# Tap products of the last convolution block in a bank of the common pool, issued in four pieces between the attention heads

## The chip, the cores and the metric

The kernel runs on one NeuronCore of a Trainium2 chip. The metric is device time of one launch, in microseconds (us), lower is better. Five engines work side by side, each through its own queue, strictly in order: PE (TensorE, the matrix unit), DVE (VectorE), ACT (ScalarE), POOL (GpSimd) and SP (SyncE, which here only issues transfers). They wait for one another through semaphores, so an instruction whose operand is late also holds up all that stand behind it in its queue.

## The reference, cut to what matters

A two-layer encoder on 512 tokens of width 1024, all in float32. Each layer is a feed-forward block, a mixer, a second feed-forward block and a norm. The mixer projects the normed stream once and splits the columns between eight attention heads and a convolution module:

```python
def conv_group(u_raw, conv_w, conv_b, ln_g, ln_b):
    a, g = u_raw[..., :CONV_W], u_raw[..., CONV_W:]     # CONV_W = 512
    u = a * jax.nn.sigmoid(g)
    y = lax.conv_general_dilated(u, conv_w[:, None, :], window_strides=(1,),
        padding=[(CONV_K - 1, 0)], feature_group_count=CONV_W, ...)   # causal, depthwise, CONV_K = 31
    y = y + conv_b
    return jax.nn.silu(layer_norm(y, ln_g, ln_b))
...
x = x + jnp.concatenate([attn, conv], axis=-1) @ w_out[l]
```

The LayerNorm runs over all 512 convolution channels, so nothing of it can begin before every channel has its 31 taps summed.

## The kernel before, in words

Activations lie with channels on the 128 partitions and the 512 tokens along the free axis, so one 128x512 float32 tile holds 128 channels and fills one PSUM bank. A large product is made of three matmuls (L144, L145, L146) on a rounded high part and a remainder of each operand. ACT makes the high parts of weights (`wh`, L133) and DVE the remainders (`wl`, L139); both have rings of four tiles, and the raw weights a ring of three (`raw`), filled by SP in program order.

PSUM has eight banks. Seven form the common pool `ps`, from which `bank()` takes; a taken bank returns when its last reader is done. The eighth is a pool of its own with one tile, tag `cv`.

The convolution's 512 channels are four blocks, and the string `CONV = "DAAP"` says how each gets its 31 taps:

- Block 0, kind D: an accumulator `cv` in the eighth bank. ACT writes the first tap and the bias (L813), DVE adds the other 30 in a chain, each `scalar_tensor_tensor` reading what the one before wrote (L817), and ACT copies the result out (L827).
- Blocks 1 and 2, kind A: for each tap ACT multiplies (`pr`, L821, three buffers) and POOL adds (`y`, L825), 30 each.
- Block 3, kind P: `packed`. Sixteen small transfers make four tiles (`zs`), each with 32 channels in four copies shifted by 0 to 3 tokens (L783, after a four-column memset, L781). PE then multiplies by 128x32 tap matrices `wtap`: eight steps of four matmuls, one for each group of 32 channels, which write 32 partitions each (L787). The four of a step use separate column strips of the array. The profile counts every such float32 matmul twice. ACT adds the bias (L790). The accumulator is the same `cv` bank that block 0 uses, and `packed` comes first in the program.

The mixer goes through these stages: projections (first two weight tiles of block 0, then q latents, blocks 1 and 2, k latents, queries, keys), the eight heads, the convolution's sum and LayerNorm, the output projection. The heads are software-pipelined in steps: in each step one head is turned (q and k transposed, L695 and L700, copied by ACT L697 and DVE L702), another has its scores made (L718, mask L719, maximum on DVE L720, exponential on ACT L724), another its probabilities transposed (L739, copied out at L742), another its values (L752), and each second head its output transposed (L770). After the turn of step 1 the projection of block 3 is issued, and at the end of step 2 `packed(3)`.

POOL then sums the four blocks (L839, L840, L841; the first adds block 0 to block 1, the last adds block 3), one matmul forms the mean (L843), DVE subtracts it (L849), and the rest of the LayerNorm alternates with the first half of the output projection (L144 to L146, on attention's output).

The order of each engine's queue is not the program's. The tile framework simulates the program with its own costs and writes out a static order per engine, in which an instruction stands as early as its operands and buffers let it be in that simulation. The order thus follows from the buffers, and a change of a buffer moves instructions far away from it.

Of the kernel before, what the change touches and what calls it, by code (L numbers as in the profile page):

```python
# [7 lines left out]
FP = mybir.dt.float32  # L8
# [3 lines left out]
AF = mybir.ActivationFunctionType  # L12
# [3 lines left out]
P = 128  # L16
D = 1024
S = 512
# [52 lines left out]
def encoder_kernel(ctx: ExitStack, tc: tile.TileContext, xT, consts, vecs, rgain, wgu1, wd1,  # L71
# [9 lines left out]
    psum = ctx.enter_context(tc.tile_pool(name="psum", bufs=7, space=PSUM))  # L81
    uid = [0]

    def nm(s):
        uid[0] += 1
        return f"{s}{uid[0]}"

    def slot(dt=FP, w=S):
        return ring.tile([P, w], dt, tag="r", name=nm("r"))
# [4 lines left out]
    def bank():  # L94
        return psum.tile([P, S], FP, tag="ps", name=nm("ps"))
# [4 lines left out]
    V, A, G, T = nc.vector, nc.scalar, nc.gpsimd, nc.tensor  # L100
# [23 lines left out]
    def vv(l, name):  # L124
        o, w = VOFF[name]
        return vec[:, l, o:o + w]
# [373 lines left out]
    def mix(l, gx, norm, done):  # L500
        with tc.tile_pool(name="k", bufs=4) as kpool:
            mix_body(kpool, l, gx, norm, done)

    def mix_body(kpool, l, gx, norm, done):
        u, order = [], {}
        ys = [None if kind in "DP" else kpool.tile([P, S], FP, tag="y", name=nm("y"), bufs=2) for kind in CONV]
# [12 lines left out]
        def conv_in(c):  # L519
            pp = []  # L520
            for j in range(2):
                ps = bank()
                group(ps, load_w(wcv[l, 2 * c + j], WC, f"c{c}"), gx, range(KD), KD)
                pp.append(ps)
            glu(*pp)
# [244 lines left out]
                T.transpose(ps[:, t * P:(t + 1) * P], o[:, t * P:(t + 1) * P], ident)  # L770
            at.append(split(ps))

        def packed(c):

            w = wpool.tile([P, WC], FP, tag="raw", name=nm("raw"), bufs=3)
            nc.sync.dma_start(out=w, in_=wtap[l])
            acc = psum.tile([P, S], FP, tag="cv", name=nm("cv"), bufs=1)
            zs = []
            for g in range(4):
                t = slot()  # L780
                V.memset(t[:, 0:4], 0.0)  # L781
                for j in range(4):
                    nc.sync.dma_start(out=t[32 * j:32 * j + 32, j:S], in_=u[c][32 * g:32 * g + 32, 0:S - j])  # L783
                zs.append(t)
            for i in range(8):
                for g in range(4):
                    T.matmul(acc[32 * g:32 * g + 32, 4 * i:S], w[:, (g * 8 + i) * 32:(g * 8 + i + 1) * 32],  # L787
                             zs[g][:, 0:S - 4 * i], start=i == 0, stop=i == 7, skip_group_check=True)
            y = slot()
            A.activation(y, acc, AF.Identity, bias=cb[:, c:c + 1])  # L790
            ys[c] = y

        cw, cb = vv(l, "cw"), vv(l, "cb")
        STAGES = [({"t": turn, "s": scores, "p": turn_p, "v": values, "o": turn_out}[c], int(d)) for c, d in zip(ORDER[::2], ORDER[1::2])]
        for step in range(H + 6):
            for stage, lag in STAGES:
                if 0 <= step - lag < H:
                    stage(step - lag)
                if stage is turn and step == 1:
                    conv_in(3)  # L800
            if step == 2:
                packed(3)


        with tc.issue_after(order["keys"]):
# [1 line left out]
        for c in range(4):  # L807
# [3 lines left out]
            acc = psum.tile([P, S], FP, tag="cv", name=nm("cv"), bufs=1) if kind == "D" else ys[c]  # L811
# [44 lines left out]
        cv = []  # L856
# [224 lines left out]
```

## Time and profile before

| | us |
|---|---|
| median of three runs | 1876.25 (1876.04 to 1877.94) |
| the profiled execution | 1878.56 |
| its span, first to last instruction | 1876.4 |
| PE busy in it | 1822.6 (97%) |
| DVE busy | 1310.0 (70%) |
| ACT busy | 955.2 (51%) |
| POOL busy | 272.9 (15%) |

The mean granted clock of TensorE is 0.988 of full speed. The layers' mixers lie at about 340 to 570 us and 1270 to 1500 us of the span; their heads at about 443 to 534 and 1372 to 1464.

In a timeline row the first number is the start in us, the second the duration; then engine, source line, operation, output and inputs by the program's names, shapes, and how many instructions the row merges. A bracket at the end tells how long the engine sat idle before it and what ended that. In a table of windows each engine has its busy time and count, and PEclk is the granted clock.

### The profile page before, as it was taken

How to read it: one execution, taken by the hardware profiler on the slowest of the kernel's cores; microseconds unless marked ns; L12 is line 12 of the kernel's file. 1: busy time of each engine (PE TensorE's matmuls, PEld its weight loads, DVE VectorE, ACT ScalarE, POOL GpSimd, SP SyncE). 2: the span in 40 equal slices, each digit the busy share in tenths (PEclk: the TensorE clock that was granted, in tenths of full speed). 3: DMA queues.
4: the chain of work that ended last, by engine and by line, in shares of the span. 5: the costliest groups of instructions: out<-in, count | busy, mean ns of one | idle time of the engine just before them, and what ended most of it. 6: DMA issues, size and time to landing. Idle time of an engine off the chain costs nothing.

```text
span 1876.4 us, 22441 instructions
## 1 busy us (share of the span) xinstructions
PE 1822.6 (97%) x8640; PEld 1497.8 (80%) x8640; DVE 1310.0 (70%) x1751; ACT 955.2 (51%) x1469; POOL 272.9 (15%) x216
## 2 busy tenths in 40 slices
PE   8999999999899999999999999999989999999997
PEld 6888888887578888888877888888957788888885
DVE  8957775648658957767778667864567579578754
ACT  6534444468735644445644344443777446344441
POOL 4000000057812000000000000000686210000000
PEclk9999999999999999999999999999999999999998
DMA  8332322325115333332713332222250343423121
GB/s 288 111 124 80 112 68 67 113 84 141 29 61 165 99 104 112 101 101 66 226 65 97 97 114 89 79 81 95 77 146 12 124 107 111 127 87 120 68 68 56
DMA packets 60315, 191.10 MB, mean 102 GB/s; under 512 B 6576, under 2 KB 7728, under 8 KB 60208
## 3 DMA queue, kind: packets, MB, share of 16 engines
q1 hardware_dynamic: 56320, 176.70, 29.0%
q0 software_dynamic: 3456, 12.58, 3.6%
q8 instruction: 68, 1.11, 0.2%
q10 hardware_dynamic: 432, 0.38, 0.1%
q14 instruction: 39, 0.32, 0.1%
HBM read 185.45 MB, written 2.10 MB: 100 GB/s over the span
## 4 chain that ended last, share of the span: by engine, by line
PE 74%; issue 18%; DVE 4%; ACT 2%; POOL 2%; DMA 0%; SPq 0%; POOLq 0%; DVEq 0%; ACTq 0%
PE ps L144 22%; PE ps L146 22%; PE ps L145 22%; PE ps L752 2%; PE ps L718 2%; PE ps L365 1%; DVE wl L229 1%; PE ps L739 1%; POOL y L825 1%; PE cv L787 0%; PE ps L182 0%; DVE fr L325 0%; ACT pr L821 0%; ACT r L724 0%; PE ps L700 0%
## 5 line engine op out<-in xcount | busy, mean ns | idle before, releaser
L144 PE MATMUL ps<-wh,r 128*128 128x512 f32 (+2 forms) x1392 | 524.8, 387 | 12.2 <-ACT wh L227 8.2
L145 PE MATMUL ps<-wl,r 128*128 128x512 f32 (+2 forms) x1392 | 534.3, 386 | 0.0
L146 PE MATMUL ps<-wh,r 128*128 128x512 f32 (+2 forms) x1392 | 532.0, 385 | 0.0
L227 ACT CAST wh<-fr 128x1024 fp32r<-128x1024 f32 x256 | 269.1, 1052 | 271.8 <-PE ps L146 143.1
L144 PE MATMUL ps<-r,wh 128*128 128x512 f32 x1008 | 393.7, 396 | 0.4 <-ACT r L150 0.4
L146 PE MATMUL ps<-r,wl 128*128 128x512 f32 x1008 | 392.8, 391 | 0.5 <-POOL wl L139 0.5
L145 PE MATMUL ps<-r,wh 128*128 128x512 f32 x1008 | 392.7, 390 | 0.0
L229 DVE TENSOR_TENSOR wl<-fr,wh 128x1024 fp32r<-128x1024 f32 x256 | 314.1, 1229 | 106.1 <-ACT wh L227 105.5
L144 PEld LDWEIGHTS ps<-wh,r 128*128 128x128 f32 x1392 | 262.5, 189 | 62.4 <-ACT wh L227 8.2
L145 PEld LDWEIGHTS ps<-wl,r 128*128 128x128 f32 x1392 | 262.5, 189 | 50.6 <-issue 0.5
L146 PEld LDWEIGHTS ps<-wh,r 128*128 128x128 f32 x1392 | 262.2, 188 | 50.3
L133 ACT CAST wh<-raw 128x1024 fp32r<-128x1024 f32 (+2 forms) x150 | 148.3, 992 | 207.0 <-issue 88.9
L139 DVE TENSOR_TENSOR wl<-raw,wh 128x1024 fp32r<-128x1024 f32 (+3 forms) x134 | 160.3, 1199 | 94.8 <-ACT wh L133 93.8
L144 PEld LDWEIGHTS ps<-r,wh 128*128 128x128 f32 x1008 | 189.8, 189 | 41.7 <-issue 1.5
L145 PEld LDWEIGHTS ps<-r,wh 128*128 128x128 f32 x1008 | 190.2, 189 | 41.1 <-issue 2.0
L146 PEld LDWEIGHTS ps<-r,wl 128*128 128x128 f32 x1008 | 189.9, 188 | 41.3 <-POOL wl L139 1.3
L162 POOL TENSOR_TENSOR rtok<-vtok,minus_half 128x4 f32<-128x4 f32 x9 | 11.1, 1229 | 1094.1 <-DVE vtok L188 1094.1
L443 DVE SCALAR_TENSOR_TENSOR x<-ps,x 128x512 f32<-128x512 f32 x128 | 88.2, 689 | 111.8 <-PE ps L146 111.3
L825 POOL TENSOR_TENSOR y<-y,pr 128x509 f32<-128x509 f32 (+15 forms) x120 | 158.0, 1319 | 56.2 <-ACT pr L821 49.4
L325 DVE TENSOR_TENSOR fr<-fr,fr 128x1024 f32<-128x1024 f32 x112 | 135.7, 1224 | 7.7 <-DMA fr<-in_wgu 7.3
L355 ACT ACTIVATE e<-e,rtok 128x256 f32<-128x256 f32 x120 | 61.2, 511 | 102.6 <-DVE e L346 102.4
L341 ACT COPY e<-ps 128x512 f32<-128x512 f32 x120 | 70.4, 588 | 63.3 <-PE ps L146 63.1
(169 smaller groups left out, 1717.0 us busy)
## 6 DMA issues: line engine op xcount, KB each, us to landing
fr<-in_wgu SPq DMA_DIRECT2D x176, 512.0 KB, 3.9
raw<-in_wd SPq DMA_DIRECT2D x64, 512.0 KB, 4.2
raw<-in_wd SPq DMA_DIRECT2D x32, 384.0 KB, 3.2
raw<-in_wcv SPq DMA_DIRECT2D x16, 512.0 KB, 3.4
raw<-in_wout SPq DMA_DIRECT2D x16, 512.0 KB, 4.3
raw<-in_wgu SPq DMA_DIRECT2D x8, 512.0 KB, 4.5
fr<-in_wgu POOLq DMA_DIRECT2D x8, 512.0 KB, 6.9
raw<-in_wgu POOLq DMA_DIRECT2D x8, 512.0 KB, 7.8
```

The lines of the kernel that those rows point to most:

```text
L133: A.copy(hi[:, :w], raw[:, :w])
L139: (G if kind in POOLW.split() else V).tensor_tensor(lo[:, :w], raw[:, :w], hi[:, :w].bitcast(FP), ALU.subtract)
L144: T.matmul(o, lh, rh, start=first, stop=False, skip_group_check=free)
L145: T.matmul(o, lh, rl, start=False, stop=False, skip_group_check=free)
L146: T.matmul(o, ll, rh, start=False, stop=last, skip_group_check=free)
L227: A.copy(hi[:, :w], src[:, :w])
L229: V.tensor_tensor(lo[:, :w], src[:, :w], hi[:, :w].bitcast(FP), ALU.subtract)
L325: V.tensor_tensor(oh, ah, bh, ALU.add)
L341: A.copy(w[:, j, :N], o[j][:, :N])
L355: A.activation(out[j][:, :h], src[j][:, :h], AF.Silu, scale=r)
L443: V.scalar_tensor_tensor(x[:, m, :], pd, 0.5, x[:, m, :], ALU.mult, ALU.add)
L825: order["conv"] = G.tensor_tensor(acc[:, s:], acc[:, s:], pr[:, s:], ALU.add).ins
```

## The change

`packed` is cut in two. `prepare` loads the tap matrices and issues the memsets and the sixteen shifted copies; it is called at step 1, just after the projection of block 3, where before this stood in `packed` at step 2. Its accumulator is now `bank()`, one of the seven of the common pool, held from step 1 until the bias add. The eight tap steps are issued two at a time, at the ends of steps 3, 4, 5 and 6. Nothing else is written differently. The eighth bank, tag `cv`, is left to block 0 alone.

```diff
+        pk = {}
+
+        def packed(c, steps):
+
+            if not pk:
+                prepare(c)
+            acc, w, zs = pk["acc"], pk["w"], pk["zs"]
+            for i in steps:
+                for g in range(4):
+                    T.matmul(acc[32 * g:32 * g + 32, 4 * i:S], w[:, (g * 8 + i) * 32:(g * 8 + i + 1) * 32],
+                             zs[g][:, 0:S - 4 * i], start=i == 0, stop=i == 7, skip_group_check=True)
+            if steps[-1] < 7:
+                return
+            y = slot()
+            A.activation(y, acc, AF.Identity, bias=cb[:, c:c + 1])
+            ys[c] = y
+
-        def packed(c):
+        def prepare(c):
 
             w = wpool.tile([P, WC], FP, tag="raw", name=nm("raw"), bufs=3)
             nc.sync.dma_start(out=w, in_=wtap[l])
-            acc = psum.tile([P, S], FP, tag="cv", name=nm("cv"), bufs=1)
             zs = []
...
                     nc.sync.dma_start(out=t[32 * j:32 * j + 32, j:S], in_=u[c][32 * g:32 * g + 32, 0:S - j])
                 zs.append(t)
-            for i in range(8):
-                for g in range(4):
-                    T.matmul(acc[32 * g:32 * g + 32, 4 * i:S], w[:, (g * 8 + i) * 32:(g * 8 + i + 1) * 32],
-                             zs[g][:, 0:S - 4 * i], start=i == 0, stop=i == 7, skip_group_check=True)
-            y = slot()
-            A.activation(y, acc, AF.Identity, bias=cb[:, c:c + 1])
-            ys[c] = y
+            pk.update(acc=bank(), w=w, zs=zs)
...
-            if step == 2:
-                packed(3)
+            if step == 1:
+                prepare(3)
+            if 3 <= step < 7:
+                packed(3, (2 * step - 6, 2 * step - 5))
```

Line numbers shift: the tap matmuls are L787 before and L782 after, the memsets L781 and L797, the DVE taps L817 and L829, ACT's products L821 and L833, the bias add L790 and L787. SP's queue holds the same transfers in the same order.

The order moves at three places, shown for layer 0; layer 1 moves in the same way. The first is DVE's queue in the projections. L139 makes remainders of weights, L510, L514 and L516 the gated inputs `r` of the blocks (`r_2947` is block 0's), and `cv` is block 0's accumulator. Before:

```order
L516 TENSOR_TENSOR r_2947<-t_2945,t_2943 128x512
L139 TENSOR_TENSOR wl_3086<-raw_3082,wh_3084 128x1024
L510 TENSOR_TENSOR t_3011<-ps_2980,R_2939 128x512
L514 TENSOR_TENSOR t_3015<-ps_2949,R_2939 128x512
L139 TENSOR_TENSOR wl_3117<-raw_3113,wh_3115 128x1024
L516 TENSOR_TENSOR r_3017<-t_3015,t_3013 128x512
```

And now:

```order
L516 TENSOR_TENSOR r_2947<-t_2945,t_2943 128x512
L829 SCALAR_TENSOR_TENSOR cv_4381<-r_2947,vec,cv_4381 128x511
L829 SCALAR_TENSOR_TENSOR cv_4381<-r_2947,vec,cv_4381 128x510
L829 SCALAR_TENSOR_TENSOR cv_4381<-r_2947,vec,cv_4381 128x509
L139 TENSOR_TENSOR wl_3086<-raw_3082,wh_3084 128x1024
L829 SCALAR_TENSOR_TENSOR cv_4381<-r_2947,vec,cv_4381 128x508
L829 SCALAR_TENSOR_TENSOR cv_4381<-r_2947,vec,cv_4381 128x507
L829 SCALAR_TENSOR_TENSOR cv_4381<-r_2947,vec,cv_4381 128x506
L829 SCALAR_TENSOR_TENSOR cv_4381<-r_2947,vec,cv_4381 128x505
L510 TENSOR_TENSOR t_3011<-ps_2980,R_2939 128x512
L829 SCALAR_TENSOR_TENSOR cv_4381<-r_2947,vec,cv_4381 128x504
L139 TENSOR_TENSOR wl_3117<-raw_3113,wh_3115 128x1024
```

All 30 taps of block 0 now stand here, the last (482 columns wide) just ahead of the splits of the q latents (L157) and of the last two query weights; before, they stood between the heads, from the first scores after the tap matmuls to the last transposes.

The second place is PE's queue among the heads. `cst` is the identity of the transposes, `raw` the tap matrices, `r` after the arrow the shifted copies. Before, the 32 matmuls stand in one run, which begins so:

```order
L739 MATMUL ps_3899<-cst,r_3737 128x128
L739 MATMUL ps_3899<-cst,r_3738 128x128
L739 MATMUL ps_3899<-cst,r_3739 128x128 x2
L787 MATMUL cv_3795<-r_3796,raw_3793 32x512
L787 MATMUL cv_3795<-r_3802,raw_3793 32x512
L787 MATMUL cv_3795<-r_3808,raw_3793 32x512
L787 MATMUL cv_3795<-r_3814,raw_3793 32x512
L787 MATMUL cv_3795<-r_3796,raw_3793 32x508
```

Now the first three stand apart from the fourth, with a head's turn and scores between:

```order
L719 MATMUL ps_3834<-mneg,mrow 128x64
L782 MATMUL ps_3782<-r_3758,raw_3756 32x512
L782 MATMUL ps_3782<-r_3764,raw_3756 32x512
L695 MATMUL ps_3885<-cst,q_2814 96x128 x4
L700 MATMUL ps_3892<-cst,kn_2815 96x128 x4
L718 MATMUL ps_3899<-r_3832,r_3825 128x128
L719 LDWEIGHTS mrow
L719 MATMUL ps_3899<-mneg,mrow 128x64
L782 MATMUL ps_3782<-r_3770,raw_3756 32x512
```

In whole, the 32 stand in eight runs of 2, 1, 12, 2, 7, 4, 1 and 3, each between matmuls of the heads.

The third place is ACT's queue. `pr` are products of block 2, L697 copies a head's turned queries, L724 is the exponential. Before, fifteen products follow each other, with no exponential between, up to the bias add L790:

```order
L821 ACTIVATE pr_4536<-r_3149,vec 128x501
L821 ACTIVATE pr_4539<-r_3149,vec 128x500
L790 ACTIVATE r_3852<-cv_3795,vec 128x512
L697 ACTIVATE r_3859<-ps_3854,gqs_3632 96x512
L724 ACTIVATE r_3873,sums_3871<-ps_3868,mx_3872 128x128
L724 ACTIVATE r_3874,sums_3871<-ps_3869,mx_3872 128x384
```

Now the same products stand among the exponentials of the heads:

```order
L833 ACTIVATE pr_4527<-r_3149,vec 128x504
L697 ACTIVATE r_3965<-ps_3960,gqs_3632 96x512
L833 ACTIVATE pr_4530<-r_3149,vec 128x503
L724 ACTIVATE r_3979,sums_3977<-ps_3974,mx_3978 128x128
L724 ACTIVATE r_3980,sums_3977<-ps_3975,mx_3978 128x384
L833 ACTIVATE pr_4533<-r_3149,vec 128x502
L724 ACTIVATE r_3981,sums_3977<-ps_3976,mx_3978 128x512
L833 ACTIVATE pr_4536<-r_3149,vec 128x501
L833 ACTIVATE pr_4539<-r_3149,vec 128x500
```

The bias add now stands eight products later, just ahead of the turn of the last head, and block 0's two ACT instructions (L813, L827) stand in the projections. On PE nothing has moved from the last output transpose (L770) on: the mean's matmul follows it directly in both.

## The prediction

> **What bounds the kernel now.** I read the page first, then PE's timeline through each mixer, then the releasers of its longest waits, then the tables of windows.
>
> ```profile
> span 1876.4 us, 22441 instructions
> ...
> PE 1822.6 (97%) x8640; PEld 1497.8 (80%) x8640; DVE 1310.0 (70%) x1751; ACT 955.2 (51%) x1469; POOL 272.9 (15%) x216
> ```
>
> PE is busy for 97% of the span. A change that adds and removes no arithmetic can gain where PE waits, where its clock is low, or where it runs badly packed. In the two mixers it does all three. First the tap matmuls, PE's timeline in layer 0:
>
> ```profile
> 463.10 0.70 PE L718 MATMUL ps<-r,r 96*128 96x256 f32 x2 [1.46 <-ACT r L724]
> ...
> 470.75 1.05 PE L787 MATMUL cv<-r,raw 128*32 128x512 f32 x2
> 473.00 1.02 PE L787 MATMUL cv<-r,raw 128*32 128x512 f32 x2 [1.20 <-DMA r<-r]
> ...
> 478.06 8.79 PE L787 MATMUL cv<-r,raw 128*32 128x512 f32 x58 [0.75 <-DMA r<-r]
> 486.79 0.44 PE L739 MATMUL ps<-cst,r 128*128 128x128 f32 x2
> 488.21 0.64 PE L695 MATMUL ps<-cst,q 128*96 128x128 f32 x4 [0.98 <-ACT r L697]
> ```
>
> The tap matmuls hold PE's queue from 470.75 to 486.79, 16.04 us: each of the first three waits for its shifted copy, and whatever head could have run stands behind. Then PE waits 0.98 for ACT. Layer 1:
>
> ```profile
> 1398.01 1.04 PE L787 MATMUL cv<-r,raw 128*32 128x512 f32 x2
> ...
> 1405.56 6.84 PE L787 MATMUL cv<-r,raw 128*32 128x512 f32 x58 [1.59 <-DMA r<-r]
> 1412.33 0.44 PE L739 MATMUL ps<-cst,r 128*128 128x128 f32 x2
> 1415.80 0.64 PE L695 MATMUL ps<-cst,q 128*96 128x128 f32 x4 [3.03 <-ACT r L697]
> ```
>
> Here the block takes 1398.01 to 1412.33, 14.32 us, and the wait behind it 3.03. Then the end of the heads in both layers, PE's timeline:
>
> ```profile
> 533.55 0.66 PE L770 MATMUL ps<-cst,t 128*128 128x128 f32 x4 [0.79 <-DVE t L759]
> 537.26 2.07 PE L843 MATMUL ps<-t,onesm 128*128 128x512 f32 x2 [3.05 <-POOL t L841]
> ...
> 1467.06 2.08 PE L843 MATMUL ps<-t,onesm 128*128 128x512 f32 x2 [3.06 <-POOL t L841]
> ```
>
> PE has nothing left but the mean, and that waits for POOL's sum. What the sum waited for stands in the timelines of DVE, ACT and POOL:
>
> ```profile
> 531.85 0.72 DVE L817 SCALAR_TENSOR_TENSOR cv<-r,vec,cv 128x482 f32<-128x482 f32 x1
> ...
> 532.60 0.59 ACT L827 COPY r<-cv 128x512 f32<-128x512 f32 x1 [1.39 <-DVE cv L817]
> ...
> 533.26 1.26 POOL L839 TENSOR_TENSOR t<-r,y 128x512 f32<-128x512 f32 x1 [17.98 <-ACT r L827]
> ...
> 1463.06 1.26 POOL L839 TENSOR_TENSOR t<-r,y 128x512 f32<-128x512 f32 x1 [19.00 <-ACT r L827]
> ```
>
> POOL had blocks 1 and 2 ready 17.98 and 19.00 us earlier; the late one is block 0, whose last tap ends at 532.57. Its accumulator is the bank that the tap matmuls held until 487. Last, a table of windows:
>
> ```profile
> 377.00:412.00 35.00, 35.00 (x176) 30.05 (x175) 13.52 (x13) 19.53 (x28) 21.66 (x15) 1.00 0.22 63
> 443.00:515.00 72.00, 64.59 (x382) 43.36 (x381) 46.45 (x90) 60.35 (x123) 64.47 (x53) 0.93 0.33 81
> 500.00:510.00 10.00, 10.00 (x82) 8.77 (x80) 9.72 (x19) 9.70 (x25) 9.45 (x8) 1.00 0.01 2
> 536.00:544.00 8.00, 6.74 (x15) 4.64 (x16) 4.42 (x7) 2.76 (x6) 1.21 (x1) 0.57 0.00 0
> 1415.00:1425.00 10.00, 9.20 (x43) 6.99 (x43) 5.91 (x11) 10.00 (x26) 7.87 (x8) 0.66 0.02 7
> 1465.00:1475.00 10.00, 7.94 (x23) 5.73 (x24) 4.82 (x8) 3.55 (x6) 1.93 (x2) 0.66 0.00 0
> ```
>
> Columns after the length are PE, its weight loads, DVE, ACT, POOL, then the clock. After three of these waits the clock is 0.57 to 0.66 of full. I price that as PE's busy time times what the clock lacks.
>
> **The change part by part.**
>
> *Tap matmuls.* Price of a pass: 58 counted matmuls in 6.84 us at full clock (layer 1) is 0.118 each, so a step of four channel groups, eight counted matmuls, takes 0.94 us. A single group alone takes 1.04 to 1.05. One pass thus costs about the same whether one or four groups share it. One unbroken run would need 8 passes, 7.5 us. The eight new runs of 2, 1, 12, 2, 7, 4, 1 and 3 need 1+1+3+1+2+1+1+1 = 11 passes, 10.4 us. Against 16.04 and 14.32 that saves 5.65 and 3.9, together 9.5. Bounds: 8 passes, if neighbours overlap the broken ones, save 15.2; if each of the eight runs also pays a lone group of 1.05 more, a layer needs 18.8 and loses 7.2 in all. I take 11 passes, because the lone row is what an interrupted run looks like and the leave is clean: the run of 58 ends at 486.85 and the next transpose starts at 486.79.
>
> The Trainium skill, page "TensorEngine Tiling (Array Packing)", section "Key Properties", says that changing the tiling mode, not just the tile, drains the array; there are now sixteen such changes a layer instead of two. By that rule the upper bound is the likelier price. The row of 486.79 shows no drain that can be seen, so it stays a rival.
>
> *Shifted copies.* Where do their waits go? SP's order is the same; only the memsets that release the first one move up, in DVE's queue.
>
> ```profile
> 462.69 0.28 DVE L720 TENSOR_REDUCE mx<-ps 128x1 f32<-128x128 f32 x1
> ...
> 465.65 10.78 SPq L783 DMA_DIRECT2D r<-r  x16
> ```
>
> They now follow the maximum of 462.69, so the copies start near 463.1 instead of 465.65. That alone would take only 2.5 us off. But PE now needs the third group after a head's turn and the fourth after that head's scores and transposes, some 3 and 6 us later, when they have landed. I put this wait at 0; it is inside the saving above.
>
> *Waits behind the block.* The 0.98 and 3.03 come from ACT, where fifteen products stand in a row ahead of the bias add and the next head's copy. Each product waits for POOL:
>
> ```profile
> 485.61 0.71 ACT L821 ACTIVATE pr<-r,vec 128x500 f32<-128x500 f32 x1 [0.62 <-POOL y L825]
> ...
> 497.16 18.13 POOL L825 TENSOR_TENSOR y<-y,pr 128x495 f32<-128x495 f32 x14 [0.51 <-ACT pr L821]
> ```
>
> Now they alternate with the exponentials. Gain 4.0, and with the layer-1 wait its cold clock, 9.20 x 0.34 = 3.1: together 7.1. Bounds: 0, if ACT is late for other heads instead, and 7.1.
>
> *Block 0.* Its 30 taps move into the projections. A row of that group:
>
> ```profile
> L817 DVE SCALAR_TENSOR_TENSOR cv<-r,vec,cv x60: 681/728/755, 491.5 to 1461.6; 128x511 f32<-128x511 f32 x2, 128x510 f32<-128x510 f32 x2, 128x509 f32<-128x509 f32 x2, 128x508 f32<-128x508 f32 x2
> ```
>
> 30 x 0.728 = 21.8 us a layer. From 377 to 412 DVE is busy 13.52 of 35 us, so 35.3 are wanted: DVE is just full there and ends about where it ended. Behind the taps in its queue stand the weight remainders, the gates of blocks 1 and 2 (whose PSUM banks the k latents need) and the splits of the q latents. Rings of four remainders run ahead of PE, and PE shows no wait in the window. Cost 0 to 21.8 a layer; I take 0.5, 1.0 in all, near the lower end, since only the last query weights are made close to their use.
>
> With block 0 done by 413, POOL's sum starts when blocks 1 and 2 are through: 533.26 - 17.98 = 515.3 in layer 0, and its three adds (533.26 until the mean starts at 537.26) end near 519. The heads end at 533.55 + 0.66 = 534.2 now and at about 527.6 when 5.65 + 0.98 are gone. So PE's 3.05 + 3.06 go, and the cold clock behind them: 6.74 x 0.43 = 2.9 and 7.94 x 0.34 = 2.7. Gain 11.7. What is late next is the last head's output (0.79 before L770), which stays.
>
> *The common pool.* One bank of seven is held through four steps. Nothing of before shows a bank wait in the heads, and from 500 to 510 PE is at 10.00 of 10 with ACT at 9.70 and POOL at 9.45. The heads get shorter by 5.65 + 0.98, so ACT's 60.35 of 72 us rise to 92%. The nearest row of a wait under such load is the 1.46 at 463.10. I take one of those a layer, 3.0 in all; bounds 0 and 10 (a 3.03 like that of layer 1, with its cold clock, about 5 a layer).
>
> *Sum.* 9.5 + 7.1 + 11.7 = 28.3 gained, 1.0 + 3.0 paid: 24.3. The profiled execution took 1878.56 (span 1876.4 and 2.2 around it), 2.3 above the median; I take the difference from the median: 1876.25 - 24.3 = 1852.
>
> **The rivals.**
>
> *The heads do not shrink.* ACT's products pace them: an exponential behind a product that waits for POOL (1.30 us an add, 18.13/14) is late, and PE with it. For it: ACT at 92%, POOL at 64.47 of 72. Against it: product 500 was through at 486.3, and at 1.30 a piece product 492, ahead of the last head's turn, comes at 496.7, 30 us before the new end of the heads. Then only the 11.7 at the end stay, less 1.0: 1865.5.
>
> *The end does not shrink.* POOL's adds, held up by ACT's new order, end after the heads; the mean waits for blocks 1 and 2 instead of block 0. Against it: 8 us between 519 and the new end of the heads. Then 24.3 - 11.7: 1863.7.
>
> *Each break drains the array*, as above: the first term becomes -7.2, the gain 7.6, the time 1868.6.
>
> *Slower: the taps of block 0 land on PE's path.* In the projections PE is at 35.00 of 35, so each us by which a remainder or a bank comes too late is lost. If all 21.8 a layer were exposed, 43.6, the time would be 1876.25 + 43.6 - 25.3 = 1894.5. It decides from 25.3 of 43.6 on, when over half of the taps are exposed. Against it: the idle 21.5 of DVE in that window and the rings.
>
> *Nothing changes*, because the copies do not start earlier (SP's order is the old one). That would leave the waits of the first three groups only, and the end gains all the same.
>
> **How the numbers follow.** Forecast 0.68: 1852, its own range 1846 to 1860. Heads not shrunk 0.12 (1865.5); end not shrunk 0.08 (1863.7); drains 0.06 (1868.6); slower 0.05 (1894.5); nothing 0.01. The lowest the bounds allow is 8 passes and no new cost, 1876.25 - 34 = 1842. The range 1844 to 1865 leaves out the drains, the slower case and about half of the heads' rival. A measurement of this kernel tells about 0.2%, 3.8 us, from no change; the first four cases are faster than that: faster 0.92, same 0.03, slower 0.05.
>
> **What would show it.** L839 waits for a POOL add or for block 3, not for L827, and L843 follows L770 at once at full clock. No L782 waits for a transfer. Tap matmuls sum to about 10.4 us a layer. L695 shows no wait of 1 us for L697. PE stays at 100% from 377 to 443. Wrong it would be if PE waits in the projections for L139 or for a bank, or if L718 and L739 show waits for ACT of over 3 us a layer.

## The result, and the profile after

The changed kernel takes 1852.49 us (median of four runs, 1851.83 to 1853.55); the kernel before took 1877.07 beside it (1876.04 to 1877.94). The ratio is 0.987, with a 95% interval of 0.9853 to 0.9887. The forecast was 1852 in a range of 1844 to 1865. The profiled execution is the one of 1851.83; its span is 26.6 us shorter than the one shown of before, 2 us more than the medians differ, because the profiled run of before was 1.5 us above its median and the one of after 0.7 below.

The page of after, its span and the line of busy times:

```profile
span 1849.8 us, 22443 instructions
...
PE 1813.1 (98%) x8640; PEld 1491.5 (81%) x8640; DVE 1313.6 (71%) x1751; ACT 951.3 (51%) x1469; POOL 274.4 (15%) x216
```

PE is busy for 9.5 us less (1822.6 before) and idle for 36.7 us instead of 53.8. So a good third of the gain is time in which PE does the same work in fewer us, the rest is waits.

PE's timeline through the tap matmuls of layer 0 after the change (the count at a row's end is the profile's, two for each matmul):

```profile
462.64 0.70 PE L718 MATMUL ps<-r,r 96*128 96x256 f32 x2 [1.46 <-ACT r L724]
...
469.16 0.70 PE L718 MATMUL ps<-r,r 96*128 96x256 f32 x2 [0.18 <-ACT r L724]
469.82 1.38 PE L782 MATMUL ps<-r,raw 128*32 128x512 f32 x4
...
472.62 1.02 PE L782 MATMUL ps<-r,raw 128*32 128x512 f32 x2 [0.16 <-DMA r<-r]
476.32 2.74 PE L782 MATMUL ps<-r,raw 128*32 128x512 f32 x24
...
489.90 1.86 PE L782 MATMUL ps<-r,raw 128*32 128x496 f32 x14
...
497.80 1.01 PE L782 MATMUL ps<-r,raw 128*32 128x484 f32 x6
```

The copies' waits of over a us are gone (0.16 is the longest in layer 0, 0.24 in layer 1), and no turn of a head (L695) waits for ACT any more. From the start of each of the eight runs to the start of what follows, the tap matmuls take 10.52 us in layer 0 and 10.33 in layer 1; before they held PE for 16.04 and 14.32.

The end of the heads, PE's timeline in layer 0 and then layer 1, after the change:

```profile
525.35 0.66 PE L770 MATMUL ps<-cst,t 128*128 128x128 f32 x4 [0.78 <-DVE t L759]
525.85 1.02 PE L855 MATMUL ps<-t,onesm 128*128 128x512 f32 x2
532.19 0.94 PE L182 MATMUL ps<-ones,acc 128*128 128x1 f32 x8
...
1441.37 0.66 PE L770 MATMUL ps<-cst,t 128*128 128x128 f32 x4 [0.78 <-DVE t L759]
1441.86 1.02 PE L855 MATMUL ps<-t,onesm 128*128 128x512 f32 x2
1448.20 0.94 PE L182 MATMUL ps<-ones,acc 128*128 128x1 f32 x8
```

The mean (L855) follows the last transposes (L770) at once, and at full clock: 1.02 us instead of 2.07. POOL's timeline says why:

```profile
518.01 1.27 POOL L851 TENSOR_TENSOR t<-r,y 128x512 f32<-128x512 f32 x1
519.36 1.27 POOL L852 TENSOR_TENSOR t<-t,y 128x512 f32<-128x512 f32 x1
520.71 1.27 POOL L853 TENSOR_TENSOR t<-t,r 128x512 f32<-128x512 f32 x1
```

The sum is ready at 522, 4 us before PE comes to the mean. Block 0 was finished over 100 us earlier, in the projections. The table of windows there (busy time and count of PE, its weight loads, DVE, ACT and POOL, then the clock):

```profile
377.00:412.00 35.00, 35.00 (x181) 30.28 (x180) 33.17 (x43) 20.28 (x29) 21.27 (x15) 1.00 0.24 71
412.00:443.00 31.00, 30.36 (x175) 28.04 (x174) 25.85 (x55) 24.34 (x60) 18.55 (x17) 1.00 0.31 103
```

And PE's timeline, its one wait there in either layer:

```profile
418.15 1.05 PE L182 MATMUL ps<-ones,acc 128*128 128x1 f32 x8 [0.64 <-POOL acc L177]
...
1334.08 1.05 PE L182 MATMUL ps<-ones,acc 128*128 128x1 f32 x8 [0.63 <-POOL acc L177]
```

DVE (third busy column) goes from 13.52 to 33.17 of 35 us, and PE stays at 35.00. Behind it PE waits 0.64 and 0.63, for POOL, not for DVE.

Where the 26.6 us of the span come from is read by setting milestones of PE side by side. Of before, the rows not yet shown:

```profile
443.71 0.60 PE L695 MATMUL ps<-cst,q 128*96 128x128 f32 x4
546.64 0.94 PE L182 MATMUL ps<-ones,acc 128*128 128x1 f32 x8
1371.95 0.60 PE L695 MATMUL ps<-cst,q 128*96 128x128 f32 x4
1463.34 0.66 PE L770 MATMUL ps<-cst,t 128*128 128x128 f32 x4 [0.78 <-DVE t L759]
1475.77 0.95 PE L182 MATMUL ps<-ones,acc 128*128 128x1 f32 x8
```

And of after:

```profile
443.25 0.60 PE L695 MATMUL ps<-cst,q 128*96 128x128 f32 x4
1359.21 0.60 PE L695 MATMUL ps<-cst,q 128*96 128x128 f32 x4
```

| stretch, on PE | layer 0, us gained | layer 1 |
|---|---|---|
| from the program's start, or from the last L182 row, to the heads' first transpose | 0.46 | -1.71 |
| heads: first L695 to the end of the last L770 | 7.74 | 9.23 |
| end: from there to the first L182 | 6.25 | 5.60 |
| from the last L182 row to the end of the span | | -0.97 |

Heads 16.97, ends 11.85, 0.46 before the first heads, and 2.68 given back between and behind the mixers. The 0.46 is no gain of the change: PE was already 1.43 us ahead when the first mixer began, since in this execution it started earlier and came to full clock sooner, and in the projections of layer 0 it lost 0.97 of that. What the 2.68 are is told below.

### The profile page after: what moved, and what is told of

The parts are those of the page before. It is cut to its first block, busy times and chain, and to the rows that moved or that the text cites. A ratio compares the mean times of both kernels' runs of the same rounds, so it can differ in the third digit from the quotient of the medians.

```text
span 1849.8 us, 22443 instructions
## 1 busy us (share of the span) xinstructions
PE 1813.1 (98%) x8640; PEld 1491.5 (81%) x8640; DVE 1313.6 (71%) x1751; ACT 951.3 (51%) x1469; POOL 274.4 (15%) x216
## 4 chain that ended last, share of the span: by engine, by line
PE 72%; issue 18%; DVE 3%; POOL 3%; ACT 2%; DMA 1%; SPq 0%; POOLq 0%; DVEq 0%; ACTq 0%
PE ps L144 21%; PE ps L146 21%; PE ps L145 21%; POOL y L837 2%; PE ps L752 2%; PE ps L718 2%; PE ps L365 2%; PE ps L782 1%; PE ps L739 1%; DMA fr<-in_wgu 1%; DVE wl L229 1%; PE ps L182 1%; ACT pr L833 0%; POOL acc L177 0%; PE ps L700 0%
## 5 line engine op out<-in xcount | busy, mean ns | idle before, releaser
L133 ACT CAST wh<-raw 128x1024 fp32r<-128x1024 f32 (+2 forms) x150 | 148.1, 992 | 205.6 <-issue 89.0
L139 DVE TENSOR_TENSOR wl<-raw,wh 128x1024 fp32r<-128x1024 f32 (+3 forms) x134 | 159.1, 1190 | 67.1 <-ACT wh L133 65.9
L837 POOL TENSOR_TENSOR y<-y,pr 128x511 f32<-128x511 f32 (+14 forms) x120 | 159.1, 1326 | 66.4 <-ACT pr L833 59.8
```

What stands on the lines that cost most here:

```text
L133: A.copy(hi[:, :w], raw[:, :w])
L139: (G if kind in POOLW.split() else V).tensor_tensor(lo[:, :w], raw[:, :w], hi[:, :w].bitcast(FP), ALU.subtract)
L837: order["conv"] = G.tensor_tensor(acc[:, s:], acc[:, s:], pr[:, s:], ALU.add).ins
```

## The experiments

The theory: block 0's own bank makes the end, 11.7 us; the pieces and their packing make the heads; and a pass over the four column strips costs the same however many of them it fills. The rivals are named with each run. Diffs are against the changed kernel.

**The bank alone.**

```diff
-            if steps[-1] < 7:
+            if list(steps)[-1] < 7:
...
-            if step == 1:
-                prepare(3)
-            if 3 <= step < 7:
-                packed(3, (2 * step - 6, 2 * step - 5))
+            if step == 2:
+                packed(3, range(8))
```

> Of the change only the bank: block 3's accumulator is one of the common pool, the copies and all eight tap steps stand at step 2 as before. Theory (the end of the heads gains from the bank alone, the heads from the early copies and the pieces): the waits of 3.05 and 3.06 before the mean and the cold clock behind them go, 11.7 us, the projections cost 1 us, the block of tap matmuls stays 14 to 16 us with its waits for copies: 1877 - 11.7 + 1 = about 1866 us. Rival (block 0's taps, once out of the heads, free DVE and ACT there, so that the heads shrink without early copies too): 1852 to 1858 us.

Measured 1862.23 us (1859.52 to 1863.54), ratio 0.9921 [0.9907, 0.9934]. Between the two. PE's timeline in layer 0:

```profile
471.28 1.89 PE L782 MATMUL ps<-r,raw 128*32 128x512 f32 x2 [3.02 <-DMA r<-r]
...
479.47 6.84 PE L782 MATMUL ps<-r,raw 128*32 128x512 f32 x58 [0.45 <-DMA r<-r]
487.09 0.87 PE L739 MATMUL ps<-cst,r 128*128 128x128 f32 x6 [0.78 <-ACT r L787]
487.80 0.60 PE L695 MATMUL ps<-cst,q 128*96 128x128 f32 x4
...
532.30 0.66 PE L770 MATMUL ps<-cst,t 128*128 128x128 f32 x4 [0.79 <-DVE t L759]
532.79 1.02 PE L853 MATMUL ps<-t,onesm 128*128 128x512 f32 x2
539.14 0.95 PE L182 MATMUL ps<-ones,acc 128*128 128x1 f32 x8
```

The end comes whole from the bank: 6.18 us from the last L770's end to L182, where before had 12.43; in layer 1 6.14 for 11.77. That is 11.9 us. But the heads shrink too, by 2.4 and 4.5 us, although 31 of the 32 tap matmuls still stand in one piece (the first now stands ahead of a head's turn) and a copy's wait of 3 us stays. The waits of L695 for ACT behind the block (0.98 and 3.03) are gone; in their place PE waits 0.78 in each layer for the bias add (L787). With the bank, block 0's work leaves the heads and the order of ACT's queue changes; which of the two does it is not shown.

**The pieces alone.**

```diff
-            pk.update(acc=bank(), w=w, zs=zs)
+            pk.update(acc=psum.tile([P, S], FP, tag="cv", name=nm("cv"), bufs=1), w=w, zs=zs)
```

> Of the change only the early copies and the four pieces: the accumulator is the eighth bank again, which block 0 needs next. Theory (the pieces shrink the heads, but block 0 can't begin before the last piece): heads shorter by 7 to 8 us a layer; the last piece and its bias add end near 510 us of the span, the 30 taps take 22 us alone and 41 us between head work, so they end 10 to 25 us behind the heads, where PE waits for them: 1877 - 15 + 2 x (11 to 21) = 1884 to 1904 us, with one wait of over 10 us before the mean in each layer. Rival (the pieces carry the gain, the end is hidden by the last heads): 1860 to 1866 us.

Measured 1889.41 us (1888.56 to 1890.25), ratio 1.0069 [1.0056, 1.0081]: slower than before, as the theory had it. The heads take 84.30 and 84.28 us (90.50 and 92.05 before), 14.0 less, and then PE's timeline shows:

```profile
542.83 2.08 PE L855 MATMUL ps<-t,onesm 128*128 128x512 f32 x2 [15.87 <-POOL t L853]
```

And POOL's:

```profile
538.83 1.26 POOL L851 TENSOR_TENSOR t<-r,y 128x512 f32<-128x512 f32 x1 [19.37 <-ACT r L839]
```

The late one is block 0 again (L839 copies it out), now by 16 us, for its bank comes free only behind the last piece. The pieces bring 14 us in the heads, where no wait for ACT is left behind a tap run, and without the bank nearly twice that, 25.5 us, is lost at the ends. Some of the 14 may be block 0's: 13 of its 30 taps now run behind the heads instead of in them.

**Copies begun a step later.**

```diff
-            if step == 1:
+            if step == 2:
                 prepare(3)
```

> The change with the copies begun at step 2 instead of step 1, so that the program asks for them only one step ahead of the first piece. The tap runs are then 1, 1, 1, 13, 8 and 8 matmuls, 11 passes of 0.94 us as in the change. Theory (what hides the copies are the head matmuls that stand between the runs, not the earlier issue): 0 to 3 us more than the change, 1852 to 1855 us, no tap matmul waits over 0.5 us for a transfer. Rival (the early issue matters): the waits of before return, 3.9 us a layer, 1860 us.

Measured 1851.93 us (1850.68 to 1853.27), ratio 0.9869 [0.9855, 0.9882], the same as the change (0.987). One tap matmul waits 1.32 us for a transfer in layer 1, against the theory's bound of 0.5; none waits over 0.25 in layer 0. The theory's time stands: the early issue of the copies is worth nothing that the time shows; head matmuls between the runs hide most of their wait.

**One unbroken run, at two places.**

```diff
-            if 3 <= step < 7:
-                packed(3, (2 * step - 6, 2 * step - 5))
+            if step == 5:
+                packed(3, range(8))
```

> The change with all eight tap steps at the end of step 5: the 32 matmuls stand in one unbroken run. Theory (a pass costs 0.94 us whether one or four groups share it, so 8 passes are cheaper than 11): 2.9 us less a layer in the tap matmuls, 1852.5 - 5.8 = 1846.7 us. Rival (an unbroken run of 7.5 us holds up the heads: ACT sets its products ahead of the next head's copy and PE waits 1 to 3 us behind the run, with a cold clock, as before): 1852 to 1860 us.

> All eight tap steps at the end of step 6 instead of step 5, again one unbroken run. Theory (only the number of passes and of breaks counts, not the place): the same as at step 5, 1842 to 1845 us. Rival (nearer the end, the run or its bias add holds up the last heads or POOL's sum, which has 3 us to spare): 1846 to 1854 us, with a wait for ACT behind the run or one for POOL before the mean.

At step 5 1843.4 us (1841.84 to 1843.85), ratio 0.9822 [0.9808, 0.9835]; at step 6 1842.7 (1841.72 to 1844.56), ratio 0.9821 [0.9807, 0.9836]. Both are faster than either kernel, 9.1 and 9.8 us below the change, where I expected 5.8 of the first. PE's timeline of the run at step 5:

```profile
485.24 6.89 PE L782 MATMUL ps<-r,raw 128*32 128x512 f32 x64
492.06 0.64 PE L695 MATMUL ps<-cst,q 128*96 128x128 f32 x4
```

All 32 matmuls in 6.82 us from start to start, no wait for ACT behind them, and the mean still comes straight behind L770. The heads take 78.84 and 78.13 us, 3.9 and 4.7 less than in the change; 3.7 and 3.5 of it are the tap matmuls. Between these two places there is no difference; the number of breaks matters. So the pieces are not what helps: with the same bank, the same unbroken issue at step 2 took 1862.23 us above, with its waits for copies. What helps is that the block is asked for late, when its copies have landed.

**The price of a pass and of a break.** Across these kernels the tap runs have very different cuts, and one rule fits them within 0.1 us, the change within 0.3: 0.84 us for each pass (the matmuls of a run over four, rounded up) and 0.12 for each run. In the change the first run, of two matmuls, takes 1.31 and 1.12 instead of 0.96; why is not shown.

| kernel, one layer | runs | passes | 0.84 x passes + 0.12 x runs | measured, layer 0 and 1 |
|---|---|---|---|---|
| one run | 1 | 8 | 6.84 | 6.82, 6.82 |
| copies later | 6 | 11 | 9.96 | 9.98, 9.99 |
| the change | 8 | 11 | 10.20 | 10.52, 10.33 |
| pieces alone | 7 | 12 | 10.92 | 10.93, 10.89 |
| a second bank (below) | 8 | 13 | 11.88 | 11.88, 11.89 |

To separate packing from breaking, the loops over steps and groups were exchanged in the unbroken run:

```diff
-            for i in steps:
-                for g in range(4):
+            for g in range(4):
+                for i in steps:
```

> The unbroken run of 32 tap matmuls at step 5 with its two loops exchanged: all eight steps of one group of 32 channels, then the next group, so that neighbours use the same column strip. Theory (a pass costs 0.85 us with four groups in it and 0.95 alone): 32 passes of 0.85 to 0.95 against 8 of 0.85, 20 to 24 us more a layer, 1843.4 + 41 to 47 = 1884 to 1890 us. Rival (what made the broken runs dear are the breaks, and matmuls on one strip overlap too): the run stays 7 to 10 us, 1843 to 1850 us.

Measured 1873.72 us (1872.21 to 1874.69), ratio 0.9985 [0.9976, 0.9994], below both numbers of the theory and far above the rival. PE's timeline:

```profile
485.45 22.11 PE L782 MATMUL ps<-r,raw 128*32 128x512 f32 x64
```

The run takes 22.04 us from start to start: 0.69 for each matmul on one strip, against 0.84 for four of them on four strips. So packing is worth a factor of 3.2 here. My bounds were too high, since I had priced a lone matmul by rows of isolated ones, 0.95 us, which hold a break as well.

**A second bank held.**

```diff
+            A.activation(tiny("hold", 1), pk["hold"][:, 0:1], AF.Identity, bias=y[:, 0:1])
...
             pk.update(acc=bank(), w=w, zs=zs)
+            pk["hold"] = bank()
+            V.memset(pk["hold"][:, 0:1], 0.0)
```

> The change with a second bank of the common pool held for as long as block 3's: one column of it is set to zero at step 1 and read after the bias add. Theory (banks don't limit the heads: the only new wait of the change was 0.18 us): within 2 us of the change, 1851 to 1855 us, no new wait over 0.5 us in the heads. Rival (the common pool is at its limit and the change took the last free bank): the price that was forecast for one bank comes now, 1.5 to 5 us a layer, 1855 to 1862 us.

Measured 1860.16 us (1858.65 to 1861.11), ratio 0.9911 [0.9894, 0.9927]: 7.7 us more than the change, the rival's time. PE's timeline:

```profile
463.87 0.70 PE L718 MATMUL ps<-r,r 96*128 96x256 f32 x2 [2.22 <-ACT r L724]
...
1383.53 1.22 PE L718 MATMUL ps<-r,r 96*128 96x256 f32 x2 [2.21 <-ACT r L724]
```

The wait at the early scores must be one for a bank that an exponential has to read first, since the scores take nothing else from L724; it grows from 1.46 to 2.22. That is 1.5 us over both layers. The tap runs, cut otherwise by the new order, cost 1.4 and 1.6 more, together 2.9. The heads are 3.3 and 4.6 longer in all; what is left, some 3.5, fits the clock, which is at half for 3.4 and 6.8 us behind the two waits and was full there in the change. So the pool is at its edge at the early scores, but only a fifth of the price is the bank wait itself. Block 3's own bank adds nothing to that wait: it is 1.46 in the kernel before too, and in the change the first tap matmul comes behind it (469.82 against 462.64). The second bank is written from 456.20 on, by the memset, so the experiment asks more of the pool than a second bank used like block 3's would.

**Twice the taps.** The zero `zt` is one column.

```diff
                 if kind == "D":
                     V.scalar_tensor_tensor(acc[:, s:], u[c][:, :S - s], tap(k), acc[:, s:], ALU.mult, ALU.add)
+                    V.scalar_tensor_tensor(acc[:, s:], u[c][:, :S - s], zt, acc[:, s:], ALU.mult, ALU.add)
```

> The change with each of block 0's 30 taps on DVE followed by a second one of the same size that multiplies by zero, 21.8 us more on DVE in each layer's projections. It measures the cover of the taps: DVE has 1.8 of 35 us idle between 377 and 412 us in the change, and 5 of 31 us from there to the heads. Theory (the cover is used up): all but some 7 us of it is late for the query splits and the weight remainders that stand behind it, PE waits 5 to 20 us a layer, 1862 to 1892 us. Rival (the rings of remainders and the idle time of DVE around it take it in): under 2 us a layer, 1852 to 1856 us.

Measured 1877.38 us (1875.53 to 1878.35), ratio 1.0003 [0.9994, 1.0012]: 24.9 us more than the change, 12.5 a layer of the 21.8 added, inside the theory's range, but not at its place. The table of windows:

```profile
377.00:412.00 35.00, 35.00 (x180) 30.25 (x178) 33.22 (x42) 20.43 (x30) 21.00 (x15) 1.00 0.24 71
412.00:443.00 31.00, 31.00 (x180) 28.57 (x178) 30.89 (x63) 23.38 (x58) 16.26 (x15) 1.00 0.28 88
```

And PE's timeline behind it:

```profile
445.85 0.37 PE L695 MATMUL ps<-cst,q 128*96 128x128 f32 x1 [2.85 <-DVE q L640]
...
451.50 0.42 PE L700 MATMUL ps<-cst,kn 128*96 128x128 f32 x1 [3.47 <-DVE scp L666]
```

DVE is as busy as in the change in the first window and full in the second (30.89 of 31 us, 25.85 in the change), and PE still doesn't lose a tenth of a us there: the remainders and splits of the projections are in time. Late are the normed queries and keys (L640, L666) that the first heads transpose, and behind them the early scores, whose wait grows from 1.46 to 4.11 and 3.66. In all PE waits some 9.5 us a layer longer at the first heads; the rest of the 12.5 is not traced, but the clock is at half there for 17.1 us in layer 0 and 13.7 in layer 1. The cover of the change's own taps is thus real, and by an estimate it ends 9 to 12 us of DVE work behind them (21.8 less 12.5, or less 9.5).

**Block 0 copied out by DVE.** The new wait of 0.64 and 0.63 at L182 stood in no step of the prediction with this releaser. Tried on the change, and together with the run at step 6:

```diff
-                A.copy(u[c], acc)
+                V.tensor_copy(u[c], acc)
```

> The change with block 0's accumulator copied out by DVE instead of ACT. Theory (the 0.64 and 0.63 us that PE now waits for POOL's sum of squares at the q latents come from ACT's copy of block 0, 0.57 us, which stands ahead of the square in ACT's queue): both waits fall below 0.2 us, the time by about 1 us, 1851 to 1852 us. Rival (POOL's third product sum ahead of it is what is late): the waits stay at 0.6 us, 1852 to 1853 us.

> The unbroken run at the end of step 6, with block 0's accumulator copied out by DVE. Theory: the two changes add, 1842.7 - 1 = 1841 to 1842 us. Rival (the copy costs DVE, which is full there, as much as ACT gains): 1842.5 to 1844 us.

Measured 1853.39 us (1852.6 to 1854.15), ratio 0.9874 [0.9861, 0.9888], and 1843.39 us (1841.89 to 1844.23), ratio 0.982 [0.9807, 0.9834]: no gain in either. PE's timeline in the first:

```profile
419.51 1.05 PE L182 MATMUL ps<-ones,acc 128*128 128x1 f32 x8 [0.81 <-POOL acc L177]
```

The theory falls: without ACT's copy the wait grows from 0.64 to 0.81. The rival falls too, though the wait stayed. POOL's timeline in the change:

```profile
414.86 3.24 POOL L177 TENSOR_TENSOR acc<-acc,t 128x512 f32<-128x512 f32 x2 [2.16 <-ACT t L176]
```

POOL stands idle for 2.16 us ahead of its sums of squares (2.40 with the copy on DVE) and waits for ACT's squares (L176), so its product sums are not what is late. ACT has no gap there in either kernel: with the copy gone from its queue, a weight's high part (L133, 0.83 us) stands ahead of the first square in its place.

## Why the prediction was right

By its own steps; the median came out at 1852.5 for 1852.

- *Tap matmuls*, forecast 10.4 us a layer and 9.5 saved: 10.52 and 10.33, 9.5 saved. The sum was right and its parts were not. A packed pass costs 0.84, not 0.94 (the 58 counted matmuls of the row were eight passes, not seven and a quarter), and each run 0.12 besides. Some 2 us of the saving in layer 0 are clock: the run of 58 took 8.79 there and 6.84 in layer 1. The prediction gave the Trainium skill's rule in "TensorEngine Tiling (Array Packing)", section "Key Properties", that a change of tiling mode drains the array. The runs show a price for a break, 0.12 us for the way in and out together, 1 us a layer: a ninth of the 8.4 that the upper bound had (18.8 less 10.4). That the 0.12 is a drain no run shows.
- *Shifted copies*, forecast 0: 0.16 and 0.24. Right, and the earlier issue is not the reason. (The waits of before stood at the second to the fourth matmul, not at the first three.)
- *Waits behind the block*, forecast 4.0 and 3.1 of cold clock: both waits are gone. The size of the waits was right. The cause, ACT's products spread among the exponentials by the pieces, is not the only one: the pieces alone remove both waits, and the bank alone leaves 0.78 a layer in their place.
- *Block 0*, forecast 1.0 for the taps and 11.7 for the end: 0.64 and 0.63 of waits, and 11.85. In all PE loses 0.97 and 1.05 in the projections. None of it is a wait for DVE; PE waits for POOL's sum of squares (L177), and that for ACT's squares. ACT's copy of block 0 is not the reason; what else in ACT's queue is stays open.
- *The common pool*, forecast 3.0: the term that was mis-sized. The new wait a layer is 0.18 us, not 1.46. A 1.46 at the first scores was there before and stayed.
- *What no step had*: the 2.7 us given back, and some 1.6 us of cold clock in layer 0 of before, behind the wait of 463.10, that the change's run did not have. In the table of windows of before:

```profile
463.00:471.00 8.00, 7.90 (x35) 5.35 (x36) 4.48 (x14) 7.89 (x22) 5.38 (x5) 0.79 0.56 117
```

7.90 us of PE at a clock of 0.79 lack 1.6; after the change the clock is 1.00 there. Without the 3.0 for the pool and with this, the heads gave 17.0 where 13.6 was the sum; the 2.7 took most of the surplus back. (The measured parts, 9.5 + 7.1 + 1.6 less two waits of 0.18, would make 17.8; the 0.8 between is not traced.) The close hit owes that much to two errors that cancel, and it is a hit on the medians, which differ by 24.6 for 24.3; the two profiles differ by 26.6.

The rival "the heads do not shrink" falls: they shrank by 17.0. "The end does not shrink" falls, with 4 us to spare on POOL. "The taps land on PE's path" falls for the change's taps, and the doubled ones show where it would have begun. What the forecast missed most is an option: it had "8 passes, 7.5 us" as its lower bound and took the pieces as given, though one late run is both unbroken and behind its copies.

Two of the signs that it named did not come: tap matmuls still wait for a transfer, if only for 0.16 and 0.24, and PE is not at 100% from 377 to 443.

Of the 2.7 us, 1.05 go in layer 1's projections (0.63 of it at L182) and 0.14 behind its mixer; 0.42 come back between; the other 1.9 are the clock. At the norm between the layers PE waits 4.01 us for DVE in both kernels. Tables of windows, before and then after, 9 us from 2 us behind the wait on:

```profile
992.00:1001.00 9.00, 9.00 (x38) 7.34 (x37) 9.00 (x11) 3.98 (x7) 0.00 (x0) 0.89 0.19 58
```

```profile
977.50:986.50 9.00, 9.00 (x33) 7.28 (x32) 9.00 (x12) 3.12 (x5) 0.00 (x0) 0.78 0.18 58
```

The same wait and the same work, but a clock of 0.78 instead of 0.89 behind it, and five matmuls fewer in the same 9 us. The lead over before drops there from 14.46 to 13.36 us. At the last norm, after equal waits of 2.23, L182 runs 1.05 us before and 1.87 after:

```profile
1862.36 1.05 PE L182 MATMUL ps<-ones,acc 128*128 128x1 f32 x8 [2.23 <-DVE acc L177]
```

```profile
1834.93 1.87 PE L182 MATMUL ps<-ones,acc 128*128 128x1 f32 x8 [2.23 <-DVE acc L177]
```

That is 0.8. Neither stretch holds anything of the change; the last section shows what the clock behind a wait hangs on.

## What to carry to other kernels

When a shared buffer is split off, ask first which chain of work starts with its release: here the bank alone moved 30 taps by over 100 us and carried half of the gain, while the pieces without it made the kernel slower. Breaking a packed run into pieces is not free (a started pass and 0.12 us a break); if its operands are late, issue the whole run later rather than in parts. Before an effect is put down to an edit, run that edit alone, also when the sum of the forecast fits.

## What the runs showed of the hardware

The clock behind a short wait does not follow from the wait's length. The wait of 1.46 us at the early scores (L718) occurs with the same length in both layers of before, of the change and of eight of the variants, 20 times. Ten times half clock followed, ten times full clock; in before once each, in the change twice full, with the bank alone twice half. A table of windows of 1 us behind this wait in layer 0 of the unbroken run at step 5 (it ended at 463.58):

```profile
463.58:464.58 1.00, 1.00 (x4) 0.83 (x5) 1.00 (x3) 1.00 (x4) 0.74 (x1) 0.79 0.81 160
464.58:465.58 1.00, 1.00 (x2) 0.21 (x2) 0.37 (x2) 1.00 (x4) 0.09 (x1) 0.50 0.94 188
465.58:466.58 1.00, 1.00 (x5) 0.55 (x4) 0.27 (x1) 1.00 (x4) 1.00 (x1) 0.50 0.93 217
466.58:467.58 1.00, 1.00 (x6) 0.95 (x5) 0.42 (x1) 1.00 (x4) 0.16 (x2) 0.51 0.71 204
```

The clock falls 0.6 us after the wait and is back 3.4 us later (0.42 + 1 + 1 + 0.98 us at half). The same 3.4 us stand behind all eight of the ten where no further wait came in between; only the start shifts, from 0.5 to 1.8 us behind the wait. The Trainium skill, "TensorE: Matmul & The Clock Gate", section "What's actually happening", describes a window of some 3.4 us that runs free of the program. The length and the shift agree with it. Its table names a whole idle window as what brings the low clock, and there the runs differ: 1.46 us of idling were enough, ten times in 20. In one run half clock followed a wait of only 0.81 (L182 in layer 1, with the copy on DVE).

Which of the two comes can be read from a trace afterwards. In every run the stretches at half clock start on a grid of 3.413 us: in before there are seven, from 464.94 to 1864.41, a distance of 410 steps, and all lie within 0.01 us of the grid. Windows laid on two of them are at half clock throughout:

```profile
464.94:468.35 3.41, 3.41 (x15) 2.76 (x13) 1.31 (x7) 3.41 (x11) 2.42 (x2) 0.50 0.55 117
1417.26:1424.08 6.82, 6.82 (x26) 4.75 (x24) 4.68 (x10) 6.82 (x18) 5.36 (x5) 0.50 0.00 1
```

On its run's grid, each of the ten waits with half clock behind it ended 1.57 to 2.88 us behind a grid point, and each of the ten others 0.09 to 1.39 or 2.93 to 3.27 us. So the place of the wait in the grid parts the twenty cases, and the grid lies differently against the program in each run. For a forecast such a wait has a price of 0 to 1.7 us (an estimate, half of 3.4) on top of its own length, and 1 us of difference somewhere in a span is no sign of an edit.

A matmul on 32 columns costs 0.69 us among others of its strip and 0.95 where it stands alone between other work; four on four strips cost 0.84. The difference of the first two, 0.26, is more than the 0.12 of a break; what makes up the rest no run shows.
